# Branch A's attention: three of eight units of each group turned by VectorE's 32x32 blocks and a DMA through DRAM instead of by TensorE

## The chip, the cores and the metric

The kernel runs on one core of one Trainium2 chip. Its time is the device time of one execution in microseconds (us); 2126.03 us is the median of three runs before the change (2126.02 to 2127.18).

The engines that matter here are TensorE (PE in the profile: matrix products and transposes, with its weight loads on a row of their own, PEld), VectorE (DVE), ScalarE (ACT), GpSimd (POOL), SyncE (SP, which issues most DMAs) and the DMA queues. Tiles lie in on-chip memory (SBUF) and products are summed in PSUM banks of 128 x 512 floats.

## The reference, cut to what matters

One layer with two token mixers, for a sample of 512 tokens and a prompt of 1024 tokens, 1024 channels wide. Branch A is attention with eight query heads of 64 in two groups, each group sharing one head of keys and values:

```python
z = rmsnorm(x) @ W_in        # q_A k_A v_A q_B k_B v_B gate_A gate_B
q, k = rope(headnorm(q_A)), rope(headnorm(k_A))
s   = einsum('bqkgd,bskd->bkgqs', q_block, k) * 64**-0.5    # 128 queries at a time
p   = softmax(s, axis=-1)
o_a = einsum('bkgqs,bskd->bqkgd', p, v)
mix = (sigmoid(gate_A) * (o_a @ W_pA) + sigmoid(gate_B) * (o_b @ W_pB)) @ W_out
x   = x + mix
x   = x + relu(rmsnorm(x) @ W_up)**2 @ W_down
```

All of it is in 32-bit floats. The kernel gets a float product out of TensorE's rounded operands by splitting an operand into a rounded part (`hi`) and the remainder (`lo`): a product of two split operands is three matmuls (`mm3`), hi x hi, hi x lo and lo x hi.

## The kernel before, in words

The program walks through the sample first, then the prompt, then the two-matrix block behind both. Inside one sequence (`N` is 0 for the sample, 1 for the prompt) branch A goes group by group: a phase `phR` projects, normalises and rotates queries, keys and values, and a phase `phA` does the attention. Branch B (`phB`), the output projections and the rest follow. In the profile of before, the prompt's two `phA` phases lie at about 460 to 600 us and 640 to 780 us.

In `phA` of the prompt the work is cut into eight units of 512 queries (4 heads x 2 query blocks, numbered 0 to 7 below). A unit has

- four score tiles (`s_tile`, j = 0 to 3), each of 128 queries x 1024 keys: four matmuls of 512 columns into a PSUM tile `s` of two banks (two such tiles exist), a maximum over the row on DVE, the exponential on ACT with the row's sum as a by-product, the reciprocal on DVE, and the scaling of the row on POOL. The result is `p`, 128 queries x 1024 keys in SBUF (eight such buffers).
- eight key blocks (kc = 0 to 7). The second product needs keys on the partitions, so for each block TensorE transposes the 128 x 128 piece of each of the four `p` tiles into one PSUM bank `pT` (128 keys x 512 queries); ACT copies the bank as `hi`, DVE subtracts to get `lo`, and two matmuls (`pv`) of 512 columns add both into the output bank `o`, two blocks later (`LAG = 2`).

`pT`, `o` and the gate's product take turns in a pool of four PSUM banks. In the course of one unit's blocks TensorE also does the next unit's score tiles (at blocks 0, 1, 3 and 4) and, block by block, three matmuls of another product, the gate's columns (`fill.pull(1)`; `fill` is a Python generator that emits three matmuls for each step; what is left of it at the end of a group is emitted by `fill.drain()`). Loads of the gate's weights (`raw_gs`) come over the SP queue and are split into `w_gs` by ACT and DVE. When a unit's last `pv` is out, `finish_o` adds the two halves of `o` (`ot` on ACT, `os` on DVE), and `put` stores the sum.

The order of the instructions on each engine is set by a scheduler when the kernel is built; where the code says `tc.keep_in_program_order(op)`, the instruction stays behind those before it that are held in the same way. Before the change nothing in the prompt's `phA` is held. `mul` and `mm3` hold their matmuls whenever the list `held_pe` isn't empty, which before is so only in a part of branch B. `put` issues a store at once, on ACT's queue, as long as `slot_no[0]` is `None`; with a number there it keeps the store in a list, `later_put`, until the program issues it on SP's queue.

Branch B already turns a part of its probabilities without TensorE, and its rows are used below: `pbs` is turned in 32x32 blocks by DVE (L1100), written to DRAM (`tbs`), fetched (`bhs`), and `bhs` is rounded by ACT (L1122) and DVE (L1123). Its exponential (L1088) writes runs of 32 where the tile is turned in this way, and single floats four apart where it is not.

## Time and profile before

| | before |
|---|---|
| median of three runs | 2126.03 us (2126.02 to 2127.18) |
| time of the profiled execution | 2126.34 us |
| span of the profiled execution | 2124.5 us |
| PE busy | 2096.5 us, 99% of the span |
| PEld busy | 1839.0 us, 87% |
| DVE busy | 1480.0 us, 70% |
| ACT busy | 1145.7 us, 54% |
| POOL busy | 363.3 us, 17% |

The span is the time from the first to the last instruction on the chip; the execution's own time is 1.84 us longer. In rows of groups of instructions, "A<-B" is what an instruction writes and reads, then come the shape in partitions x elements, the number of instructions after an x, the busy time with the mean of one in ns, and behind the second bar the engine's idle time just before such instructions with what ended it. In rows of the timeline the first number is the start in us and the second the duration; matmuls overlap in PE's pipe, so that the pace of a row of them is the distance of their starts. L12 is line 12 of the kernel.

### The profile page before, as it was taken

Reading aid. Unit: us, or ns where it says so; the run is one execution under the profiler, and the core shown is the slowest. Engines: PE = TensorE matmul, PEld = TensorE weight load, DVE = VectorE, ACT = ScalarE, POOL = GpSimd, SP = SyncE. Lnnn points to the kernel's source line nnn. Section 1 sums busy time; section 2 is a strip of 40 time slices with the busy share of each in tenths; the row PEclk is TensorE's granted clock in tenths of the full one; section 3 lists DMA queues with packets and bytes.
Section 4 is the critical chain, followed back from the end, with each engine's and each line's share of the span. In section 5 each row is a group of like instructions: output and inputs, shape, how many; then the busy total and the mean of one; then the engine's idle time right before and its main releaser. Section 6 shows DMA issues by size and latency. Waiting matters only on the chain.

```text
span 2124.5 us, 31728 instructions
## 1 busy us (share of the span) xinstructions
PE 2096.5 (99%) x10871; PEld 1839.0 (87%) x10871; DVE 1480.0 (70%) x2793; ACT 1145.7 (54%) x2487; POOL 363.3 (17%) x446
## 2 busy tenths in 40 slices
PE   9999999999999999999999999999999999999998
PEld 8888778888898888887888999999999988888887
DVE  6666786777647756777873877778777777669563
ACT  6665653666666745556531566666565643334452
POOL 2232310332232314443101100002000000000000
PEclk9999999999999999999999999999999999999999
DMA  6436557530122136876563656568454899688561
GB/s 191 133 99 200 160 150 256 192 86 23 49 70 87 45 84 193 241 224 193 172 227 124 199 181 206 163 230 214 156 162 146 272 350 341 213 280 278 164 204 64
DMA packets 336104, 372.92 MB, mean 176 GB/s; under 512 B 31039, under 2 KB 267207, under 8 KB 335943
## 3 DMA queue, kind: packets, MB, share of 16 engines
q1 hardware_dynamic: 297463, 305.60, 45.6%
q10 hardware_dynamic: 31328, 45.11, 6.2%
q0 software_dynamic: 7152, 20.19, 3.5%
q8 instruction: 86, 1.41, 0.3%
q14 instruction: 75, 0.61, 0.1%
HBM read 274.29 MB, written 97.32 MB: 175 GB/s over the span
## 4 chain that ended last, share of the span: by engine, by line
PE 52%; DVE 1%; issue 0%; ACT 0%; POOLq 0%; POOL 0%; ACTq 0%; DVEq 0%
PE dn L212 20%; PE ua L212 6%; PE ud L212 6%; PE uc L212 6%; PE ops L212 4%; PE ub L212 3%; PE ppbs L212 2%; PE ppas L212 2%; PE dnf L212 2%; PE pt L353 1%; PE obs L212 0%; PE ptbs L1132 0%; ACT pbs L1088 0%; PE sbs L212 0%; DVE A L1458 0%
## 5 line engine op out<-in xcount | busy, mean ns | idle before, releaser
L212 PE MATMUL dn<-wd,ah 128*128 128x512 f32 x1248 | 384.2, 389 | 0.0
L212 PEld LDWEIGHTS dn<-wd,ah 128*128 128x128 f32 x1248 | 234.2, 188 | 48.7
L212 PE MATMUL dn<-wd,al 128*128 128x512 f32 x624 | 242.8, 389 | 0.0
L1457 ACT ACTIVATE ah<-ar 128x512 fp32r<-128x512 f32 x168 | 104.4, 627 | 206.7 <-PE dn L212 185.6
L212 PE MATMUL gpss<-xs_0h,w_gs 128*128 128x512 f32 x512 | 189.4, 402 | 0.8 <-DVE ot_Bs L471 0.4
L1458 DVE TENSOR_TENSOR al<-ar,ah 128x512 fp32r<-128x512 f32 x168 | 114.1, 687 | 76.4 <-ACT ah L1457 66.6
L212 PE MATMUL ud<-B,A 128*128 128x384 f32 x768 | 143.7, 334 | 0.7 <-DVE c L1575 0.7
L212 PE MATMUL uc<-B,A 128*128 128x384 f32 x768 | 143.7, 334 | 0.0
L212 PE MATMUL ua<-B,A 128*128 128x384 f32 x768 | 138.8, 334 | 0.0
L212 PEld LDWEIGHTS dn<-wd,al 128*128 128x128 f32 x624 | 117.1, 188 | 24.2
L794 POOL TENSOR_SCALAR ps<-ps,rls 128x1024 f32<-128x1024 f32 (+1 forms) x96 | 96.8, 1009 | 228.4 <-DVE rls L793 213.8
L212 PEld LDWEIGHTS ud<-B,A 128*128 128x128 f32 x768 | 134.0, 188 | 1.1 <-DVE c L1575 1.1
L212 PEld LDWEIGHTS uc<-B,A 128*128 128x128 f32 x768 | 134.1, 188 | 0.2 <-ACT A L1457 0.2
L834 ACT ACTIVATE pths<-pTs 128x512 fp32r<-128x512 f32 x160 | 94.1, 597 | 73.9 <-PE pTs L829 71.3
L212 PEld LDWEIGHTS ua<-B,A 128*128 128x128 f32 x768 | 133.7, 188 | 0.2
L835 DVE TENSOR_TENSOR ptls<-pTs,pths 128x512 fp32r<-128x512 f32 x160 | 107.5, 686 | 37.7 <-ACT pths L834 36.7
L212 PE MATMUL ops<-wh_os,mgs 128*128 128x512 f32 x384 | 119.4, 390 | 0.0
L788 DVE TENSOR_REDUCE nms<-ss 128x1 f32<-128x1024 f32 (+1 forms) x96 | 99.8, 1040 | 25.0 <-PE ss L786 24.5
L212 PEld LDWEIGHTS gpss<-xs_0h,w_gs 128*128 128x128 f32 x512 | 96.1, 188 | 19.0 <-DVE w_gs L206 0.7
L791 ACT ACTIVATE ps<-ss,nms 128x1024 f32<-128x1024 f32 (+1 forms) x96 | 93.3, 972 | 32.1 <-DVE nms L788 26.2
L180 POOL TENSOR_TENSOR rs_f<-ms_f,mhalf 128x1 f32<-128x1 f32 x6 | 4.0, 667 | 590.7 <-DVE ms_f L176 590.7
L829 PEld LDWEIGHTS pTs<-ident,ps 128*128 128x128 f32 x640 | 78.0, 140 | 28.4 <-POOL ps L794 4.4
(287 smaller groups left out, 5144.2 us busy)
## 6 DMA issues: line engine op xcount, KB each, us to landing
ar<-ud SPq DMA_DIRECT2D x120, 512.0 KB, 5.4
br<-in_w_mlp_down_dram SPq DMA_DIRECT2D x72, 512.0 KB, 5.3
rawu<-in_w_mlp_up_dram SPq DMA_DIRECT2D x64, 512.0 KB, 4.1
ud<-c ACTq DMA_DIRECT2D x128, 192.0 KB, 3.6
raw_gs<-in_w_in_dram SPq DMA_DIRECT2D x32, 512.0 KB, 3.9
ud<-cs SPq DMA_DIRECT2D x64, 192.0 KB
tbs<-pbs SPq DMA_DIRECT2D x24, 384.0 KB, 4.8
bhs<-tbs SPq DMA_DIRECT2D x24, 384.0 KB, 3.7
```

Source lines behind the costliest of these rows:

```text
L180: nc.gpsimd.tensor_tensor(r[:, :n], m[:, :n], mhalf[:, :n], op=ALU.pow)
L212: op = nc.tensor.matmul(out, a, b, **kw)
L353: nc.tensor.transpose(halves[c // 4][:, (c % 4) * P : (c % 4 + 1) * P], t[:, c * P : (c + 1) * P], ident)
L788: nc.vector.tensor_reduce(nm_, s, axis=AX.X, op=ALU.max, negate=True)
L791: op = nc.scalar.activation(p, s, AF.Exp, bias=nm_, accum_out=l)
L794: nc.gpsimd.tensor_scalar(p, p, rl, 1.0, op0=ALU.mult, op1=ALU.mult)
L829: nc.tensor.transpose(pt[:, j * P : (j + 1) * P], PP[u, j][:, kc * P : (kc + 1) * P], ident)
L834: nc.scalar.activation(hi, pt, AF.Copy)
L835: nc.vector.tensor_tensor(lo, pt, hi.bitcast(F32), op=ALU.subtract)
L1457: nc.scalar.activation(hi, src, AF.Copy)
L1458: nc.vector.tensor_tensor(lo, src, hi.bitcast(F32), op=ALU.subtract)
```

## The change

In both groups of the prompt, units 1, 3 and 5 are "turned": TensorE no longer transposes their probabilities. For such a unit

- the exponential reads the scores in another order, with a step of four floats in PSUM, and writes runs of 32 floats, so that the 32x32 blocks come to lie side by side (L798 to L803 of the changed kernel);
- DVE turns each of the four 128 x 1024 tiles in place in 32x32 blocks (`turn`, L832), and SP stores the tile to DRAM (512 KB, L834);
- SP fetches it again in another order of partitions (`fetch`, 512 KB, L841), which completes the transposition;
- ACT makes the rounded copy (128 x 1024, L848, not before the last exponential issued so far), and the remainder is formed in place (L850), for tiles j = 0 and 2 on POOL, for j = 1 and 3 on DVE (`rounded`);
- `pv_pair` takes two tiles at a time: 16 matmuls of 256 columns for each of a unit's two halves.

So five units have their eight blocks: `step` for units 0, 2, 4, 6 and 7, and `between_steps` where a turned unit is. In `between_steps` TensorE does the four score tiles of the unit after, the last two `pv` of the unit before, four steps of the gate's product and the first half of the turned unit; the second half comes at block 1 of the following step. The score tiles of a turned unit are done at blocks 0 to 3 of the step before it. All of TensorE's matmuls of the phase are held in program order, and so are DVE's turns, SP's stores and fetches, and the subtractions of `rounded`. A `p` buffer now holds two tiles, and four such pairs are shared by `p` and the fetched `fa`. The outputs' stores go by `later_put` on SP's queue. Nothing changes for the sample and for the rest but line numbers.

The diff, with `pv`, `end_o`, the issue of the late stores and what only changes how functions are called left out:

```diff
 ...
@@ -772,9 +772,10 @@
                 setup_bias()
             with phase(f"phA{N}_{g}") as ph:
                 units = [(h, qb) for h in range(4) for qb in range(NB)]
-                PP = {}
-
-                def s_tile(u, j):
+                PP, tA, fA, hA, pairs, last_exp = {}, {}, {}, {}, {}, [None]
+                turned = {units[i] for i in (1, 3, 5)} if NB == 2 else set()
+
+                def s_tile(u, j, between=None):
                     h, qb = u
                     nm = f"{N}_{g}_{h}_{qb}_{j}"
                     q0 = (qb * 4 + j) * P
 ...
-                    p = ph.tile([P, T], F32, tag="P", name=f"p{nm}", bufs=8)
+                    if between is not None:
+                        between()
+                    if NB == 1:
+                        p = ph.tile([P, T], F32, tag="P", name=f"p{nm}", bufs=8)
+                    else:
+                        if j % 2 == 0:
+                            pairs[u, j // 2] = ph.tile([P, 2, T], F32, tag="P", name=f"p{nm}", bufs=4)
+                        p = pairs[u, j // 2][:, j % 2]
                     l = sml.tile([P, 1], F32, tag="l", name=f"l{nm}")
-                    op = nc.scalar.activation(p, s, AF.Exp, bias=nm_, accum_out=l)
+                    to, of = p, s
+                    if u in turned:
+                        to = p.rearrange("p (b k i) -> p k b i", b=4, i=32)
+                        of = s.rearrange("p (k i b) -> p k b i", b=4, i=32)
+                    op = nc.scalar.activation(to, of, AF.Exp, bias=nm_, accum_out=l)
+                    last_exp[0] = op.ins
                     rl = sml.tile([P, 1], F32, tag="rl", name=f"rl{nm}")
                     nc.vector.reciprocal(rl, l)
                     nc.gpsimd.tensor_scalar(p, p, rl, 1.0, op0=ALU.mult, op1=ALU.mult)
 ...
+                def turn(u, j):
+                    p = PP[u, j]
+                    blocks = p.rearrange("p (n i) -> p n i", i=32)
+                    tc.keep_in_program_order(nc.vector.transpose(blocks, blocks))
+                    tA[u, j] = dram.tile([P, 4, T // 4], F32, name=f"ta{N}_{g}_{u[0]}_{u[1]}_{j}")
+                    tc.keep_in_program_order(nc.sync.dma_start(tA[u, j], p.rearrange("p (b w) -> p b w", b=4)))
+
+                def fetch(u, j):
+                    of = tA.pop((u, j)).rearrange("(a i) b w -> (i b) a w", i=32)
+                    if j % 2 == 0:
+                        fA[u, j // 2] = ph.tile([P, 2, T], F32R, tag="P", name=f"fa{N}_{g}_{u[0]}_{u[1]}_{j}", bufs=4)
+                    to = fA[u, j // 2][:, j % 2].bitcast(F32).rearrange("p (a w) -> p a w", a=4)
+                    tc.keep_in_program_order(nc.sync.dma_start(to, of))
+
+                def rounded(u, j, eng):
+                    if j % 2 == 0:
+                        hA[u, j // 2] = slot([P, 2, T], F32R, f"ha{N}_{g}_{u[0]}_{u[1]}_{j // 2}")
+                    p, hi = fA[u, j // 2][:, j % 2], hA[u, j // 2][:, j % 2]
+                    with tc.issue_after(last_exp[0]):
+                        nc.scalar.activation(hi, p.bitcast(F32), AF.Copy)
+                    tc.keep_in_program_order(
+                        eng.tensor_tensor(p, p.bitcast(F32), hi.bitcast(F32), op=ALU.subtract)
+                    )
+
+                def pv_pair(u, pr):
+                    if pr == 0:
+                        o_of[u] = mm(f"o{N}_{g}_{u[0]}_{u[1]}")
+                    o = o_of[u][:, pr * 256 : pr * 256 + 256].rearrange("p (n i) -> p n i", i=32)
+                    hi, lo = hA.pop((u, pr)), fA.pop((u, pr))
+                    for kc in range(NT):
+                        for i, t in enumerate((hi, lo)):
+                            mv = t.rearrange("p j w -> p (j w)").rearrange("p (n k i) -> p k n i", n=8, i=32)[:, kc]
+                            mul(
+                                o,
+                                vhl[:, kc, :],
+                                mv,
+                                start=(kc + i == 0),
+                                stop=(kc + i == NT),
+                                skip_group_check=True,
+                            )
+                    if pr == 1:
+                        end_o(u)
+
+                if NB == 2:
+                    held_pe.append("A")
+                    slot_no[0] = 0
 ...
+                def put_later():
+                    slot_no[0] += 1
+                    while later_put and later_put[0][0] < slot_no[0] - 1:
+                        nc.sync.dma_start(*later_put.pop(0)[1:])
+
+                def step(u, nxt, late, pulls):
+                    h, qb = u
+                    moving = nxt in turned
+                    if moving:
+                        after = {4: [partial(fetch, nxt, 0)], 5: [partial(turn, nxt, 3), partial(fetch, nxt, 1)]}
+                        after[7] = [partial(fetch, nxt, 2), partial(rounded, nxt, 0, nc.gpsimd)]
+                    for kc in range(NT):
+                        pt = mm(f"pT{N}_{g}_{h}_{qb}_{kc}")
+                        for j in range(4):
+                            op = nc.tensor.transpose(
+                                pt[:, j * P : (j + 1) * P], PP[u, j][:, kc * P : (kc + 1) * P], ident
+                            )
+                            tc.keep_in_program_order(op)
+                        hi = ph.tile([P, 512], F32R, tag="pth", name=f"pth{N}_{g}_{h}_{qb}_{kc}", bufs=3)
+                        lo = ph.tile([P, 512], F32R, tag="ptl", name=f"ptl{N}_{g}_{h}_{qb}_{kc}", bufs=3)
+                        nc.scalar.activation(hi, pt, AF.Copy)
+                        nc.vector.tensor_tensor(lo, pt, hi.bitcast(F32), op=ALU.subtract)
+                        queue.append((u, kc, hi, lo))
+                        if nxt is not None:
+                            at = (0, 1, 2, 3) if moving else (0, 1, 3, 4)
+                            if kc in at:
+                                j = at.index(kc)
+                                s_tile(nxt, j, partial(turn, nxt, j - 1) if moving and j else None)
+                            for f in after.get(kc, ()) if moving else ():
+                                f()
+                        fill.pull(pulls[kc])
+                        if kc == 1 and late is not None:
+                            pv_pair(late, 1)
+                        if len(queue) > LAG:
+                            pv(*queue.pop(0))
+                        if kc % 4 == 3:
+                            put_later()
+
+                def between_steps(u, nxt):
+                    s_tile(nxt, 0)
+                    pv(*queue.pop(0))
+                    fetch(u, 3)
+                    s_tile(nxt, 1)
+                    pv(*queue.pop(0))
+                    fill.pull(2)
+                    s_tile(nxt, 2, partial(rounded, u, 1, nc.vector))
+                    fill.pull(1)
+                    rounded(u, 2, nc.gpsimd)
+                    s_tile(nxt, 3)
+                    fill.pull(1)
+                    rounded(u, 3, nc.vector)
+                    pv_pair(u, 0)
+                    put_later()
+
+                if NB == 2:
+                    for i in (0, 2, 4):
+                        step(units[i], units[i + 1], units[i - 1] if i else None, (1,) * 8)
+                        between_steps(units[i + 1], units[i + 2])
+                    step(units[6], units[7], units[5], (2, 1, 1, 1, 1, 1, 1, 2))
+                    step(units[7], None, None, (2, 1, 1, 1, 1, 1, 1, 2))
 ...
```

What this makes of the engines' orders is shown at two places. Names end in sequence, group, head, query block and tile or key block: `ps_0_1_1_2` is tile 2 of group 0, head 1, query block 1, which is unit 3, a turned one; unit 2 is `0_1_0` and unit 4 is `0_2_0`. `ps` is the scaled tile, `nms` the row maximum, `rls` the reciprocal, `ptls` the remainder of a transposed block; `fas` and `has` are the fetched and the rounded tile. After the change two tiles share a buffer that is named for the first, so that `ps_0_1_1_0` stands for tiles 0 and 1, and `fas_0_1_1_0` likewise.

The first is the step of unit 2, in which the tiles of unit 3 are made. DVE there, before:

```order
L788 TENSOR_REDUCE nms_0_1_1_1_6061<-ss_0_1_1_1_6056 128x1
L793 RECIPROCAL rls_0_1_1_0_6039<-ls_0_1_1_0_6037 128x1
L483 TENSOR_TENSOR os_As_0_0_1_6076<-os_0_0_1_5923,ot_As_0_0_1_6074 64x512
L835 TENSOR_TENSOR ptls_0_1_0_2_6085<-pTs_0_1_0_2_6079,pths_0_1_0_2_6084 128x512
L793 RECIPROCAL rls_0_1_1_1_6066<-ls_0_1_1_1_6064 128x1
L788 TENSOR_REDUCE nms_0_1_1_2_6108<-ss_0_1_1_2_6103 128x1
L835 TENSOR_TENSOR ptls_0_1_0_3_6100<-pTs_0_1_0_3_6094,pths_0_1_0_3_6099 128x512
L835 TENSOR_TENSOR ptls_0_1_0_4_6124<-pTs_0_1_0_4_6118,pths_0_1_0_4_6123 128x512
L788 TENSOR_REDUCE nms_0_1_1_3_6132<-ss_0_1_1_3_6127 128x1
```

and now:

```order
L806 RECIPROCAL rls_0_1_1_0_5991<-ls_0_1_1_0_5989 128x1
L832 STREAM_TRANSPOSE ps_0_1_1_0_5988<-ps_0_1_1_0_5988 128x1024
L806 RECIPROCAL rls_0_1_1_1_6018<-ls_0_1_1_1_6016 128x1
L483 TENSOR_TENSOR os_As_0_0_1_6042<-os_0_0_1_5955,ot_As_0_0_1_6040 64x512
L902 TENSOR_TENSOR ptls_0_1_0_2_6050<-pTs_0_1_0_2_6044,pths_0_1_0_2_6049 128x512
L789 TENSOR_REDUCE nms_0_1_1_2_6058<-ss_0_1_1_2_6053 128x1
L832 STREAM_TRANSPOSE ps_0_1_1_0_5988<-ps_0_1_1_0_5988 128x1024
L902 TENSOR_TENSOR ptls_0_1_0_3_6081<-pTs_0_1_0_3_6075,pths_0_1_0_3_6080 128x512
L806 RECIPROCAL rls_0_1_1_2_6066<-ls_0_1_1_2_6064 128x1
L789 TENSOR_REDUCE nms_0_1_1_3_6089<-ss_0_1_1_3_6084 128x1
L832 STREAM_TRANSPOSE ps_0_1_1_2_6063<-ps_0_1_1_2_6063 128x1024
L902 TENSOR_TENSOR ptls_0_1_0_4_6112<-pTs_0_1_0_4_6106,pths_0_1_0_4_6111 128x512
```

The turns now stand between the remainders of the blocks; the turn of tile 0 stands ahead of the remainder of block 2, the turn of tile 1 ahead of that of block 3, and that of tile 2 ahead of block 4's.

The second place is `between_steps` at unit 3. POOL there; before:

```order
L794 TENSOR_SCALAR ps_0_1_1_3_6134<-ps_0_1_1_3_6134,rls_0_1_1_3_6137 128x1024
L794 TENSOR_SCALAR ps_0_2_0_0_6203<-ps_0_2_0_0_6203,rls_0_2_0_0_6206 128x1024
L794 TENSOR_SCALAR ps_0_2_0_1_6234<-ps_0_2_0_1_6234,rls_0_2_0_1_6237 128x1024
L794 TENSOR_SCALAR ps_0_2_0_2_6281<-ps_0_2_0_2_6281,rls_0_2_0_2_6284 128x1024
L794 TENSOR_SCALAR ps_0_2_0_3_6305<-ps_0_2_0_3_6305,rls_0_2_0_3_6308 128x1024
```

and now:

```order
L850 TENSOR_TENSOR fas_0_1_1_0_6115<-fas_0_1_1_0_6115,has_0_1_1_0_6171 128x1024
L807 TENSOR_SCALAR ps_0_2_0_0_6187<-ps_0_2_0_0_6187,rls_0_2_0_0_6190 128x1024
L807 TENSOR_SCALAR ps_0_2_0_0_6187<-ps_0_2_0_0_6187,rls_0_2_0_1_6205 128x1024
L807 TENSOR_SCALAR ps_0_2_0_2_6232<-ps_0_2_0_2_6232,rls_0_2_0_2_6235 128x1024
L850 TENSOR_TENSOR fas_0_1_1_2_6169<-fas_0_1_1_2_6169,has_0_1_1_1_6241 128x1024
L807 TENSOR_SCALAR ps_0_2_0_2_6232<-ps_0_2_0_2_6232,rls_0_2_0_3_6253 128x1024
```

Two subtractions of 128 x 1024 now stand on POOL among the scalings of unit 4's tiles, the second of them ahead of the scaling of tile 3.

DVE there; before, while unit 4's tiles 2 and 3 are made:

```order
L835 TENSOR_TENSOR ptls_0_1_1_2_6256<-pTs_0_1_1_2_6250,pths_0_1_1_2_6255 128x512
L835 TENSOR_TENSOR ptls_0_1_1_3_6271<-pTs_0_1_1_3_6265,pths_0_1_1_3_6270 128x512
L788 TENSOR_REDUCE nms_0_2_0_2_6279<-ss_0_2_0_2_6274 128x1
L835 TENSOR_TENSOR ptls_0_1_1_4_6295<-pTs_0_1_1_4_6289,pths_0_1_1_4_6294 128x512
L788 TENSOR_REDUCE nms_0_2_0_3_6303<-ss_0_2_0_3_6298 128x1
L793 RECIPROCAL rls_0_2_0_2_6284<-ls_0_2_0_2_6282 128x1
L835 TENSOR_TENSOR ptls_0_1_1_5_6325<-pTs_0_1_1_5_6319,pths_0_1_1_5_6324 128x512
```

and now:

```order
L789 TENSOR_REDUCE nms_0_2_0_2_6228<-ss_0_2_0_2_6223 128x1
L806 RECIPROCAL rls_0_2_0_1_6205<-ls_0_2_0_1_6203 128x1
L483 TENSOR_TENSOR os_As_0_1_0_6212<-os_0_1_0_6072,ot_As_0_1_0_6210 64x512
L850 TENSOR_TENSOR fas_0_1_1_0_6115<-fas_0_1_1_0_6115,has_0_1_1_0_6171 128x1024
L806 RECIPROCAL rls_0_2_0_2_6235<-ls_0_2_0_2_6233 128x1
L789 TENSOR_REDUCE nms_0_2_0_3_6249<-ss_0_2_0_3_6244 128x1
L806 RECIPROCAL rls_0_2_0_3_6253<-ls_0_2_0_3_6251 128x1
L850 TENSOR_TENSOR fas_0_1_1_2_6169<-fas_0_1_1_2_6169,has_0_1_1_1_6241 128x1024
```

Of unit 3's blocks, one `ptls` for each, nothing is left here; the maximum of unit 4's tile 3 stands behind the remainder of the fetched tile 1, and the reciprocal of tile 2 ahead of that maximum. TensorE does one step of the gate's product and the first half of unit 3 between unit 4's last score tile and the first transposes that read it, where before blocks 4 to 7 of unit 3 stood.

28 lines of the change are left out of this document (19 added, 9 removed).

## The prediction

> **What bounds the kernel now.** I read the page's busy shares and chain of waits first, then windows inside the two phases that change, then the waits of TensorE there, and last the timeline.
>
> ```profile
> span 2124.5 us, 31728 instructions
> PE 2096.5 (99%) x10871; PEld 1839.0 (87%) x10871; DVE 1480.0 (70%) x2793; ACT 1145.7 (54%) x2487; POOL 363.3 (17%) x446
> 480.00:500.00 20.00, 20.00 (x109) 16.36 (x108) 14.94 (x24) 13.31 (x24) 5.41 (x5) 1.00 0.07 21
>   DVE os_As L483: 3.1, 12
>   POOL ps L794: 2.0, 5
>   DVE ptls L835: 1.0, 4
> ```
>
> TensorE is busy in the whole of the 20 us window (PE is its first figure, then PEld, DVE, ACT, POOL, the granted clock, which is full, and DMA's share), with DVE at 14.94 us second. The last three rows are what ended the waits of the transposes (L829) from 440 to 780 us, both phases together: 6.1 us. So TensorE's own work sets the pace, a matmul saved there is time saved, and any wait that the change brings is time lost.
>
> **What leaves TensorE.**
>
> ```profile
> 480.66 0.60 PE L829 MATMUL pTs<-ident,ps 128*128 128x128 f32 x4
> 481.01 0.48 PE L785 MATMUL ss<-kTs,qTs 128*128 128x512 f32 x1
> 481.33 0.40 PE L786 MATMUL ss<-kTs,qTs 128*128 128x512 f32 x1
> 481.56 0.40 PE L785 MATMUL ss<-kTs,qTs 128*128 128x512 f32 x1
> 481.80 0.40 PE L786 MATMUL ss<-kTs,qTs 128*128 128x512 f32 x1
> 482.03 0.39 PE L212 MATMUL gpss<-xs_0h,w_gs 128*128 128x512 f32 x1
> 864.73 0.89 PE L212 MATMUL obs<-bhs,vss 128*128 128x256 f32 x6
> 865.45 0.87 PE L212 MATMUL sbs<-kBs,qBs 128*128 128x384 f32 x4
> ```
>
> Starts tell the pace. The four transposes of a block take 481.01 - 480.66 = 0.35 us; the matmul behind them 0.32 where the others take 0.23; a block's transposes thus cost 0.35 + 0.09 = 0.44. Six turned units have 48 blocks: -21.1 us. Their second product becomes 32 matmuls of 256 columns instead of 16 of 512. Six of 256 take 865.45 - 864.73 = 0.72, so 0.12 each: 32 x 0.12 - 16 x 0.2315 = +0.14 a unit, +0.8 us. Net **-20.3 us**, or 3.4 for a pair of an unturned and a turned unit; that is what a pair may wait before nothing is won.
>
> **What comes onto DVE and POOL.**
>
> ```profile
> L835 DVE TENSOR_TENSOR ptls<-pTs,pths 128x512 fp32r<-128x512 f32 x160 | 107.5, 686 | 37.7 <-ACT pths L834 36.7
> L788 DVE TENSOR_REDUCE nms<-ss 128x1 f32<-128x1024 f32 x64 | 77.9, 1217 | 17.6 <-PE ss L786 17.5
> L1100 DVE STREAM_TRANSPOSE pbs<-pbs 128x768 f32<-128x768 f32 x24 | 23.2, 966 | 0.0
> L1123 DVE TENSOR_TENSOR bhs<-bhs 128x768 fp32r<-128x768 f32 x24 | 23.1, 964 | 9.9 <-ACT bhs L1122 9.7
> L834 ACT ACTIVATE pths<-pTs 128x512 fp32r<-128x512 f32 x160 | 94.1, 597 | 73.9 <-PE pTs L829 71.3
> L791 ACT ACTIVATE ps<-ss,nms 128x1024 f32<-128x1024 f32 x64 | 71.3, 1115 | 21.3 <-DVE nms L788 15.4 <-DMA vds<-vts 3.1 <-DVE rls L793 2.5
> L794 POOL TENSOR_SCALAR ps<-ps,rls 128x1024 f32<-128x1024 f32 x64 | 73.6, 1150 | 170.2 <-DVE rls L793 167.0 <-PE pTs L829 3.2
> L365 POOL TENSOR_TENSOR B<-ta,B 128x512 fp32r<-128x512 f32 x12 | 15.5, 1294 | 120.6 <-ACT B L362 120.2
> L685 POOL TENSOR_TENSOR us<-ts,rts 128x160 f32<-128x160 f32 x48 | 29.3, 632 | 56.3 <-issue 30.0 <-DVE vhls L677 20.2 <-DVE ts L676 6.1
> ```
>
> By length, a turn of 1024 takes 0.966 x 1024/768 = 1.29 and a subtraction on DVE 1.28. A turned unit gives DVE four turns and two subtractions for eight remainders of 0.69: +7.7 - 5.5 = +2.2 us. A pair keeps its TensorE work else: 16 blocks at 0.44 + 0.46, eight score tiles at 0.93 and twelve gate steps of three matmuls at 0.69 are 30.1 us before, and 26.8 now. DVE has 14.94/20 x 30.1 = 22.5 before, some 24.7 now: from 75% to 92%. It still fits, but nothing on it can be late for long. A subtraction of 1024 on POOL isn't in the trace; its two nearest rows give (1.294 - 0.632)/352 = 1.88 ns a column and so 1.294 + 512 x 0.00188 = 2.26; in proportion to either row it is 2.6 or 4.0, at the scalings' pace 1.15. I take 2.3, as the row of 512 is nearest.
>
> **The wait inside a step** (three of a group's steps make a turned unit's tiles). Two of four PSUM banks are free for `pT`, since `o` and the gate's product hold the others: block k's transposes wait for the remainder of block k-2.
>
> ```profile
> 482.54 1.22 DVE L788 TENSOR_REDUCE nms<-ss 128x1 f32<-128x1024 f32 x1
> 483.67 0.15 DVE L793 RECIPROCAL rls<-ls 128x1 f32<-128x1 f32 x1
> 485.73 0.16 DVE L793 RECIPROCAL rls<-ls 128x1 f32<-128x1 f32 x1 [0.40 <-ACT ps L791]
> 486.06 1.12 POOL L794 TENSOR_SCALAR ps<-ps,rls 128x1024 f32<-128x1024 f32 x1 [0.95 <-DVE rls L793]
> ```
>
> Now the first turn stands ahead of block 2's remainder. From the step's start it can't begin before 6.7 us: remainder 0 and maximum 0 end at 3.2, the exponential (behind ACT's second copy) at 4.5, maximum 1 and the reciprocal at 5.3, and the scaling runs from 0.33 later for 1.1. To block 4's remainder DVE then has turn 1.29, reciprocal 0.16, `os` 0.68, remainder 0.69, maximum 1.22, turn 1.29, remainder 0.69, reciprocal 0.16, maximum 1.22, turn 1.29, remainder 0.69: 9.4, or 8.7 since an instruction starts some 0.08 before the stated end of the one ahead (482.54 + 1.22 against 483.67). It ends at 15.4 to 16.1. Block 6's transposes wait for it, and TensorE would reach them at 14.3 (six blocks with four tiles, six gate steps, four `pv` and 1.93 for half a turned unit): 1.1 to 1.8, and I take 1.2. In a group's first step that half unit and the `os` are missing: TensorE is there at 12.3, the remainder at 14.7 to 15.4, and I take 2.7. Without this late turn both would be 0. Sum 4 x 1.2 + 2 x 2.7 = **+10.2 us**.
>
> **The wait between steps.** Here the last score tile S3 of the next unit is followed on TensorE by only one gate step (0.69) and half a turned unit (1.93), and then by block 0's transposes, the fourth of which reads S3's scaled tile. Counting from the end of tile S2 on: DVE maximum 2 to 1.2, reciprocal 1, `os` to 2.1, the subtraction of fetched tile 1 to 3.3, reciprocal 2 to 3.5, so that S2's scaling goes from 3.7 to 4.8 on POOL. Then POOL's second subtraction stands ahead of S3's scaling: to 7.1, and that scaling to 8.3. TensorE has gate 0.69, S3 0.93, gate 0.69 and the half 1.93, with the start of the next row in its pipe 4.4. The wait is 3.9; the three pairs of a group differ by which reciprocal stands behind which subtraction (3.3, 3.8, 4.6 by the same walk), so 4.0 x 6 = **+24 us**. Below, only S3's own chain remains (maximum 1.22, exponential and reciprocal 1.23, scaling 0.33 + 1.12 with hand-overs, 4.4 from S3's last matmul against 3.2 of work): 1.15 x 6 = 7. Above, 5 x 6 = 30, if POOL's and DVE's subtractions of two SBUF tiles hinder each other:
>
> ```profile
> 811.52 1.18 POOL L1091 TENSOR_SCALAR pbs<-pbs,rlbs 128x384 f32<-128x384 f32 x2 [1.26 <-DVE rlbs L1090]
> 826.70 1.84 POOL L1091 TENSOR_SCALAR pbs<-pbs,rlbs 128x384 f32<-128x384 f32 x2 [1.77 <-DVE rlbs L1090]
> 827.12 0.97 DVE L1123 TENSOR_TENSOR bhs<-bhs 128x768 fp32r<-128x768 f32 x1
> ```
>
> Two scalings take 1.18 alone and 1.84 beside such a subtraction: +0.66. [...]
>
> **What is hidden, and the end.** A store and a fetch of 512 KB each pass on SP between TensorE's blocks:
>
> ```profile
> raw_gs<-in_w_in_dram SPq DMA_DIRECT2D x3, 512.0 KB, 4.2
> tbs<-pbs SPq DMA_DIRECT2D x24, 384.0 KB, 4.8
> bhs<-tbs SPq DMA_DIRECT2D x24, 384.0 KB, 3.7
> ```
>
> At 4.2 each the first fetched tiles land some 9 us after their turns (7 to 13 us into the step), in time for the copies behind the next unit's first exponential; the DMA share was 0.07. ACT loses 56 rows and isn't late; On SP each fetch waits for its tile's store; behind it stand the next stores, the outputs' stores moved here, which nothing in the phase reads, and loads of the gate's weights, which come a column block ahead. The gate's steps run out after block 2 of a group's last unit; its five blocks are then bound by transposes, copy 0.60 and remainder 0.69, about 1 us a group more: +2.
>
> **Sum.** 2124.5 - 20.3 + 24 + 10.2 + 2 = 2140.4; with 2126.34 - 2124.5 = 1.84 around the span 2142.2, and the profiled execution lies 0.31 above the median: 2142.
>
> **Rivals.** *The waits are small* (the other side): TensorE's saving stays and only S3's own chain is waited for. It speaks for it that DVE and POOL are idle at times and that the walk adds up gaps which overlap; against it that both orders above are held. 2126 - 20.3 + 7 = 2113 with steps at 0. It decides when a pair waits under 3.4. *No change*: a pair waits about 3.4 in all (say 2.5 between and 0.9 in the step), 2126. *The strided exponential*: a turned unit's exponential reads every fourth float of PSUM.
>
> ```profile
> L1088 ACT ACTIVATE pbs<-sbss,nmbs 128x384 f32<-128x384 f32 x14 | 13.7, 996 | 7.4 <-DVE nmbs L1059 7.3
> L1088 ACT ACTIVATE pbs<-sbss,nmbs 128x384 f32<-128x384 f32 x50 | 31.1, 625 | 19.4 <-DMA tbs<-pbs 13.0 <-issue 2.8 <-DVE nmbs L1059 2.8
> ```
>
> From 985 to 1050 us branch B's exponential writes single floats four apart and takes 0.996, from 780 to 985 it writes runs of 32 and takes 0.625: +0.37 for 384 floats, so +1.0 for 1024. The tile's turn would be later by that, and the step's wait by about 1 a pair: +6, 2148. For the rest reads may differ from writes, and no row has such a read. [...] *Late fetches*: at 4.9 a transfer, the copies on ACT stand late ahead of the next exponential; 0.75 a pair, +4.5, 2146.5.
>
> **Chances.** The forecast's mechanism, waits in both places above the saving (2131 to 2150), has 0.50; the small waits 0.19; no change 0.11; the strided exponential 0.13; late fetches 0.07. About 0.2%, or 4.3 us, can be told from no change; so faster 0.19, same 0.11, slower 0.70. The range reaches down to 2116, into the small waits, and up to 2152, where the strided read and hindered subtractions come together; the likeliest case's own is 2131 to 2150.
>
> **What would show it.** Right: 96 matmuls of 128x256 more and 96 transposes fewer in a group, at 0.12 each and 0.44 a block; first transposes of units 2, 4, 6 idle 3 to 5 us with POOL's scaling as releaser; in steps, transposes idle with DVE's remainder as releaser, and the turns late by POOL. Wrong: PE still 99% busy in both phases; a POOL subtraction near 1.2; the exponential of turned units near 2 us; transposes released by a DMA.

## The result: slower by 1.7%, more than twice what was forecast

| | before | with the change |
|---|---|---|
| median | 2126.61 us (2126.02 to 2127.59, 4 runs) | 2163.35 us (2160.54 to 2164.4, 4 runs) |
| ratio | | 1.0170 (95%: 1.0153 to 1.0188) |
| span of the profiled execution | 2124.5 us | 2161.7 us |

The kernel became 36.7 us slower. The forecast was 2142 us (2116 to 2152): the direction was right, but the time lies above the range, and the loss is 37 us where 16 were forecast. The spans differ by 37.2 us.

The profile's page of the changed kernel, first rows of the busy times:

```profile
span 2161.7 us, 31545 instructions
PE 2092.8 (97%) x10775; PEld 1835.1 (85%) x10775; DVE 1499.9 (69%) x2781; ACT 1143.7 (53%) x2463; POOL 403.9 (19%) x458
```

TensorE is no longer busy throughout. The two phases in windows, first before, then with the change (columns as before: length, PE, PEld, DVE, ACT, POOL, granted clock, DMA share, GB/s):

```profile
453.00:580.00 127.00, 126.17 (x676) 102.90 (x676) 92.70 (x147) 84.08 (x149) 36.98 (x32) 1.00 0.14 43
640.00:780.00 140.00, 139.91 (x746) 114.78 (x745) 96.04 (x153) 88.92 (x162) 37.24 (x33) 1.00 0.21 61
```

```profile
455.00:600.00 145.00, 124.81 (x634) 102.17 (x632) 102.64 (x140) 84.36 (x136) 57.15 (x38) 0.95 0.38 124
655.00:815.00 160.00, 139.32 (x717) 114.50 (x716) 109.78 (x154) 89.15 (x151) 58.60 (x41) 0.96 0.43 136
```

Before, TensorE stood still for under 1 us in a phase, at a clock of 1.00. Now it stands still for 145 - 124.8 = 20.2 and 160 - 139.3 = 20.7 us, and the clock's mean is 0.95 and 0.96. TensorE's waits from 440 to 820 us, with what ended them, the total, the number and the longest:

```profile
PE pTs L895 <- POOL ps L807: 27.9, 10, 4.1
PE os L212 <- issue: 6.0, 6, 1.7
PE pTs L895 <- DVE ptls L902: 3.5, 6, 0.8
PE ss L212 <- ACT ps L803: 2.6, 3, 0.9
PE pTs L895 <- DVE os_As L483: 1.0, 1, 1.0
```

Of the ten waits in the first row six stand between steps and four at the groups' starts. One of the six, on TensorE, at units 3 and 4 of the first group (L212 is the helper `mul`, through which all matmuls but the transposes go):

```profile
525.26 0.28 PE L212 MATMUL os<-has,vhls 128*128 128x256 f32 x1
526.55 0.36 PE L212 MATMUL os<-fas,vhls 128*128 128x256 f32 x1 [1.01 <-issue]
...
528.43 0.49 PE L895 MATMUL pTs<-ident,ps 128*128 128x128 f32 x3
532.97 0.33 PE L895 MATMUL pTs<-ident,ps 128*128 128x128 f32 x1 [4.05 <-POOL ps L807]
```

and on POOL and DVE at the same place:

```profile
528.51 2.34 POOL L850 TENSOR_TENSOR fas<-fas,has 128x1024 fp32r<-128x1024 f32 x1
530.83 2.08 POOL L807 TENSOR_SCALAR ps<-ps,rls 128x1024 f32<-128x1024 f32 x1
...
525.24 1.20 DVE L850 TENSOR_TENSOR fas<-fas,has 128x1024 fp32r<-128x1024 f32 x1
...
528.91 0.16 DVE L806 RECIPROCAL rls<-ls 128x1 f32<-128x1 f32 x1 [1.27 <-ACT ps L803]
529.86 2.07 DVE L850 TENSOR_TENSOR fas<-fas,has 128x1024 fp32r<-128x1024 f32 x1 [0.78 <-ACT has L848]
```

Three of four transposes are out at 528.4; the fourth waits 4.05 us for the scaling of the last score tile. Its reciprocal is there at 529.1, but POOL is at its subtraction until 530.85, and then the scaling itself takes 2.08 in place of 1.12, beside a DVE subtraction that takes 2.07 in place of 1.20. That is the forecast's mechanism. Two things beside it were not in the forecast: half a turned unit waits inside itself (1.01 at 526.55, until the DVE subtraction of 525.24 is over), and what comes behind the long wait is slow. Three windows around the same wait one pair earlier, and TensorE's rows behind it:

```profile
496.00:500.00 4.00, 1.39 (x6) 1.17 (x7) 1.90 (x2) 0.60 (x1) 2.55 (x2) 0.95 0.00 0
500.00:504.00 4.00, 4.00 (x14) 3.25 (x14) 2.63 (x4) 1.69 (x3) 0.00 (x0) 0.62 0.03 6
504.00:508.00 4.00, 4.00 (x28) 3.68 (x28) 2.67 (x6) 2.40 (x4) 1.59 (x2) 1.00 0.00 0
```

```profile
499.75 0.63 PE L212 MATMUL gpss<-xs_1h,w_gs 128*128 128x512 f32 x1
500.18 0.63 PE L212 MATMUL gpss<-xs_1l,w_gs 128*128 128x512 f32 x1
```

The matmuls start 0.43 apart instead of 0.23, and the granted clock is 0.50 for some 3.4 us. Taking the windows in slices of half a microsecond and adding up (1 - clock) x busy time gives 6.8 us in the first group (four such stretches) and 5.9 in the second (three), none before.

**Where the 37.2 us are.** TensorE's idle time is 40.9 us in the two phases, against 0.9 before: +40.0. The low clock: +12.6. A wait costs more than its row says, because the idle time begins at the end of the last matmul's 0.28 to 0.39, not at the pace of 0.12 or 0.23: at 526.55 the starts lie 1.29 apart, 1.17 more than the pace, for a row of 1.01. About 0.2 for each of 26 waits of more than 0.15 is +5.2. With TensorE's saving of -20.3 as forecast the sum is 37.5. The 0.2 is an estimate from rows like this one, so the parts are good to a microsecond or two.

### The profile page after: what moved, and what is told of

Same layout as the page of the kernel before. It is cut to its first block, busy times and chain, and to the rows that moved or that the text cites. A ratio compares the mean times of both kernels' runs of the same rounds, so it can differ in the third digit from the quotient of the medians.

```text
span 2161.7 us, 31545 instructions
## 1 busy us (share of the span) xinstructions
PE 2092.8 (97%) x10775; PEld 1835.1 (85%) x10775; DVE 1499.9 (69%) x2781; ACT 1143.7 (53%) x2463; POOL 403.9 (19%) x458
## 4 chain that ended last, share of the span: by engine, by line
PE 52%; DVE 1%; issue 0%; ACT 0%; POOLq 0%; POOL 0%; ACTq 0%; DVEq 0%
PE dn L212 20%; PE ua L212 6%; PE ud L212 6%; PE uc L212 6%; PE ops L212 4%; PE ub L212 3%; PE ppbs L212 2%; PE ppas L212 2%; PE dnf L212 2%; PE pt L353 0%; PE obs L212 0%; PE gpss L212 0%; PE sbs L212 0%; PE ptbs L1263 0%; DVE A L1589 0%
## 5 line engine op out<-in xcount | busy, mean ns | idle before, releaser
L212 PE MATMUL dn<-wd,ah 128*128 128x512 f32 x1248 | 384.4, 389 | 0.0
L212 PEld LDWEIGHTS dn<-wd,ah 128*128 128x128 f32 x1248 | 234.2, 188 | 48.7
L212 PE MATMUL dn<-wd,al 128*128 128x512 f32 x624 | 242.8, 389 | 0.0
L212 PE MATMUL gpss<-xs_0h,w_gs 128*128 128x512 f32 x512 | 190.0, 405 | 0.8 <-DVE ot_Bs L471 0.4
L807 POOL TENSOR_SCALAR ps<-ps,rls 128x1024 f32<-128x1024 f32 (+1 forms) x96 | 108.7, 1134 | 197.5 <-DVE rls L806 123.6
L212 PE MATMUL ud<-B,A 128*128 128x384 f32 x768 | 143.6, 334 | 0.7 <-DVE c L1706 0.7
L212 PE MATMUL uc<-B,A 128*128 128x384 f32 x768 | 143.7, 334 | 0.0
L212 PE MATMUL ua<-B,A 128*128 128x384 f32 x768 | 138.8, 334 | 0.0
L212 PEld LDWEIGHTS dn<-wd,al 128*128 128x128 f32 x624 | 117.1, 188 | 24.3
L212 PEld LDWEIGHTS ud<-B,A 128*128 128x128 f32 x768 | 134.0, 188 | 1.0 <-DVE c L1706 1.0
L212 PEld LDWEIGHTS uc<-B,A 128*128 128x128 f32 x768 | 134.0, 188 | 0.2 <-ACT A L1588 0.2
L212 PEld LDWEIGHTS ua<-B,A 128*128 128x128 f32 x768 | 133.7, 188 | 0.2
L212 PE MATMUL ops<-wh_os,mgs 128*128 128x512 f32 x384 | 119.4, 390 | 0.0
L212 PEld LDWEIGHTS gpss<-xs_0h,w_gs 128*128 128x128 f32 x512 | 97.7, 191 | 19.9 <-DVE w_gs L206 0.7
L803 ACT ACTIVATE ps<-ss,nms 128x1024 f32<-128x1024 f32 (+1 forms) x96 | 93.3, 973 | 34.8 <-DVE nms L789 31.2
L212 PE MATMUL ss<-kTs,qTs 128*128 128x512 f32 x320 | 100.4, 429 | 5.1 <-ACT ps L803 3.3
L212 PE MATMUL gpss<-xs_0l,w_gs 128*128 128x512 f32 x256 | 101.8, 398 | 0.0
L212 PE MATMUL gpss<-xs_1h,w_gs 128*128 128x512 f32 x256 | 95.9, 410 | 0.0
```

Source lines behind the costliest of these rows:

```text
L212: op = nc.tensor.matmul(out, a, b, **kw)
L803: op = nc.scalar.activation(to, of, AF.Exp, bias=nm_, accum_out=l)
L807: nc.gpsimd.tensor_scalar(p, p, rl, 1.0, op0=ALU.mult, op1=ALU.mult)
```

## The experiments

All times are medians beside runs of the kernel before on the same chip (2126.8 to 2127.1). The theory at this point: POOL's and DVE's subtractions stand ahead of the scaling that TensorE waits for, and the wait lowers the clock behind it. The rivals: the own chain of the last score tile; the held order of TensorE; a saving that was priced too high. In the edits, `rounded(..., sub=False)` is ACT's copy alone and `rounded(..., copy=False)` the subtraction alone, which then stays behind the instruction named in the comment or in `after_`.

### POOL's second subtraction behind the scaling

```diff
-                    rounded(u, 2, nc.gpsimd)
+                    rounded(u, 2, nc.gpsimd, sub=False)      # ACT's copy only
                     s_tile(nxt, 3)
+                    rounded(u, 2, nc.gpsimd, copy=False)     # POOL, behind the scaling of tile 3
```

> The changed kernel with one instruction moved: POOL's second subtraction (fetched tile 2) is issued behind the scaling of the next unit's tile 3 instead of ahead of it. Theory (POOL's queue, then the clock): the wait of 4.05 us ahead of the next unit's first transposes loses about the subtraction's 2.35 and comes to 1.5 to 2; at that length the granted clock stays at 1.00 behind it. 6 x (2.3 + 1.7) = 24 less than 2163: 2139 (2133 to 2147). Rival (DVE and tile 3's own chain end last, POOL only happens to be the last in the row): the wait stays above 3.4 and the time at 2158 to 2164.

Measured: 2145.62 us (2142.11 to 2146.95), 17.7 less than the change. TensorE and POOL at the same place as above:

```profile
526.32 0.49 PE L902 MATMUL pTs<-ident,ps 128*128 128x128 f32 x3
528.24 0.33 PE L902 MATMUL pTs<-ident,ps 128*128 128x128 f32 x1 [1.43 <-POOL ps L808]
...
527.07 1.12 POOL L808 TENSOR_SCALAR ps<-ps,rls 128x1024 f32<-128x1024 f32 x1 [1.43 <-DVE rls L807]
528.15 3.36 POOL L855 TENSOR_TENSOR fas<-fas,has 128x1024 fp32r<-128x1024 f32 x1
```

The wait falls from 4.05 to 1.43, and the clock stays at 1.00 behind all six. POOL's subtraction is what stood in the way. A part of the gain is given back: in the last pair of each group a new wait of 3.16 and 3.08 us appears, for `os`, with a low clock behind it. DVE there has splits of weights for what follows the group, ahead of `os`; the first of them takes 2.89 and 2.88 beside POOL's late subtraction (3.37 and 3.38).

### Useless matmuls in the wait

Ahead of block 0's transposes in the steps that follow a turned unit, 16 matmuls of 512 columns are put in, whose result is overwritten:

```diff
                         pt = mm(f"pT{N}_{g}_{h}_{qb}_{kc}")
+                        if kc == 0 and late is not None:
+                            for _ in range(16):
+                                mul(pt, kT[:, 0, 0:P], kT[:, 1, 0:512], start=True, stop=True)
```

> The changed kernel with 16 matmuls of 512 columns, whose result is overwritten, ahead of the first transposes of units 2, 4, 6 and, at the group's end, of none else (about 3.7 us of TensorE's time put into the wait of 4.05). Theory (a long wait lowers the granted clock for the 3.5 us behind it): the wait falls under 1 us, the transposes start when they did, the clock stays at 1.00, and the matmuls behind run at 0.23 instead of 0.43: about 1.7 x 6 = 10 us less, 2153 (2149 to 2157), though more work is done. Rival (the slow matmuls behind the wait have another cause, or the clock falls whatever TensorE does): 2163 or more.

Measured: 2155.24 us (2154.37 to 2156.01), 8.1 less with 22 us of work more. At the first pair:

```profile
494.63 3.84 PE L212 MATMUL pTs<-kTs 128*128 128x512 f32 x16
498.31 0.49 PE L898 MATMUL pTs<-ident,ps 128*128 128x128 f32 x3
499.23 0.33 PE L898 MATMUL pTs<-ident,ps 128*128 128x128 f32 x1 [0.42 <-POOL ps L807]
499.31 1.18 PE L212 MATMUL ss<-kTs,qTs 128*128 128x512 f32 x4
500.33 0.39 PE L212 MATMUL gpss<-xs_1h,w_gs 128*128 128x512 f32 x1
500.55 0.39 PE L212 MATMUL gpss<-xs_1l,w_gs 128*128 128x512 f32 x1
```

The transpose comes no later against its surroundings, the matmuls behind it run at 0.23, and the only low clock that is left is at the first group's start. The low clock is caused by the wait and is worth 8 to 10 us of the 37.

### DVE's second subtraction out of POOL's way

```diff
-                    rounded(u, 3, nc.vector)
+                    rounded(u, 3, nc.vector, sub=False)
 ...
                         queue.append((u, kc, hi, lo))
+                        if kc == 0 and late is not None:
+                            rounded(late, 3, nc.vector, copy=False)   # behind block 0's remainder
```

> The changed kernel with one instruction moved: DVE's second subtraction (fetched tile 3) stands behind the remainder of block 0 of the next step instead of beside POOL's scaling of tile 3. Theory (the two hinder each other): the scaling of tile 3 falls from 2.1 to 1.15 us, DVE's subtraction from 2.07 to 1.2, the wait from 4.05 to 3.1: 6 us less, 2157, and 2147 if a wait of 3.1 no longer lowers the clock. Rival (the scaling is long for another reason): scaling and time as they were, 2163; or the half unit that needs this tile now waits and the time rises.

Measured: 2155.96 us (2153.91 to 2160.72). POOL and DVE at the first pair:

```profile
492.49 2.33 POOL L857 TENSOR_TENSOR fas<-fas,has 128x1024 fp32r<-128x1024 f32 x1
494.81 1.11 POOL L808 TENSOR_SCALAR ps<-ps,rls 128x1024 f32<-128x1024 f32 x1
...
497.78 1.22 DVE L855 TENSOR_TENSOR fas<-fas,has 128x1024 fp32r<-128x1024 f32 x1
```

The subtraction takes 1.22 instead of 2.07, the scaling 1.11 instead of 2.1 in four of the six pairs, and their waits are 3.07 or less. So the two do hinder each other, by 1 us a pair. In the last pair of each group the scaling stays at 2.07 and 2.08, now beside DVE's splits of weights, and the waits are 3.26 and 3.25. The time lies between the two values expected, but close to the upper: the waits between steps are 5.8 us less in all, while TensorE's idle time from 440 to 820 us falls by only 2.2 (41.4 to 39.2), since other waits grow. More of the gain is the clock's, which still falls behind three of the six waits and costs 5.8 instead of 12.6 us.

### TensorE's order held, nothing turned

`turned` is empty; all eight units go through `step`, with score tiles at blocks 0, 1, 3 and 4 and the gate steps as before the change.

```diff
-                turned = {units[i] for i in (1, 3, 5)} if NB == 2 else set()
+                turned = set()
 ...
+                    for i, u in enumerate(units):
+                        step(u, units[i + 1] if i < 7 else None, None, (1, 1, 1, 0, 1, 1, 1, 0))
```

> The changed kernel with no unit turned: eight steps of blocks as before, score tiles at blocks 0, 1, 3 and 4 and gate steps as before, but TensorE's order held, stores on SP and pairs of tiles in a buffer. Theory: holding the order costs only the waits at each group's start (2 us, with a low clock behind it in one group) and little inside: 2129 to 2134. Rival (the held order is itself what costs, since the scheduler can no longer fill gaps): over 2145.

Measured: 2132.74 us (2131.04 to 2137.45), ratio 1.0028 (1.0018 to 1.0038): the held order costs 5.6 us. (The run also keeps the stores on SP and two tiles in a buffer; no run tells their share apart.) The loss stands at the groups' starts: 4.1 us of waits, and 3.4 of low clock in the profiled execution. There TensorE waits for the scalings of tiles 2 and 3, and the clock falls behind them in both groups:

```profile
462.71 0.38 PE L895 MATMUL pTs<-ident,ps 128*128 128x128 f32 x2
464.11 0.33 PE L895 MATMUL pTs<-ident,ps 128*128 128x128 f32 x1 [1.02 <-POOL ps L807]
465.48 0.33 PE L895 MATMUL pTs<-ident,ps 128*128 128x128 f32 x1 [1.04 <-POOL ps L807]
```

Before the change the scheduler had put the next unit's score matmuls and gate steps between these very transposes:

```profile
462.99 0.38 PE L829 MATMUL pTs<-ident,ps 128*128 128x128 f32 x2
463.12 0.48 PE L785 MATMUL ss<-kTs,qTs 128*128 128x512 f32 x1
...
464.39 0.33 PE L829 MATMUL pTs<-ident,ps 128*128 128x128 f32 x1
464.47 0.47 PE L212 MATMUL gpss<-xs_1h,w_gs 128*128 128x512 f32 x1
```

### More work behind the first score tiles

```diff
                     ends = s_tile(units[0], j)
-                    fill.pull(2)
+                    fill.pull((1, 2, 1, 4)[j] if NB == 2 else 2)
```

> The changed kernel, with the gate steps behind a group's first four score tiles dealt out as 1, 2, 1, 4 instead of 2, 2, 2, 2, so that TensorE has 2.8 us of work behind the fourth tile instead of 1.4. Theory (the wait at a group's start, twice 1.02 us in each group, is tile 3's own chain against what TensorE has left): about 1.0 to 1.4 less per group, with some new wait ahead of tile 2 of 0.4, and no low clock behind it: 2163 - 2 x 0.8 - 1.7 = 2160 (2157 to 2162). Rival (the start's waits come from something else): the same two waits of 1.02, 2163.

Measured: 2161.94 us (2159.67 to 2163.74). In each group one wait of 0.92 is left of the two, as the theory had it, but the medians differ by 1.4 us where each kernel's runs spread over 4: the direction is not settled by the times.

### Everything that stands between the scaled tiles and the second product left out

```diff
                 def turn(u, j):
-                    ...
+                    pass
 
                 def fetch(u, j):
-                    ...
+                    pass
 
                 def rounded(u, j, eng):
-                    ...
+                    if (u, j // 2) not in fA:
+                        fA[u, j // 2] = hA[u, j // 2] = same[0]   # two tiles of unit 0, rounded once
```

> The changed kernel with everything left out that a turned unit needs between its scaled tiles and its second product: DVE's turns, the stores, the fetches, the rounded copies and all four subtractions (the second products read two tiles of unit 0 rounded once in place of the fetched ones, so that the outputs of units 1, 3 and 5 are not the reference's). TensorE's instructions and their order are those of the changed kernel. Theory (TensorE's saving is 20.3 us as priced, and tile 3's own chain leaves a wait of about 1.2, with some 0.2 more that a row of idle time does not show, between the steps): 2126.8 + 7.2 (start of the groups, as in the run with the order held alone) - 20.3 + 6 x 1.4 + 2 (gate steps run out at the end) = 2124 (2119 to 2129). Rival (the saving on TensorE was priced too high, and is nearer to 13): 2131 or more.

Measured: 2123.06 us (2121.33 to 2125.14), 4.0 less than the kernel before. TensorE from 440 to 820 us, which holds both phases, here and with the order held alone (the run with no unit turned, above), columns as before; this run first:

```profile
440.00:820.00 380.00, 367.11 (x2016) 316.36 (x2015) 226.33 (x416) 214.82 (x503) 111.69 (x114) 0.99 0.26 73
440.00:820.00 380.00, 374.41 (x2062) 318.72 (x2061) 247.40 (x445) 230.72 (x535) 106.92 (x108) 0.99 0.24 66
```

This run is 9.7 us shorter than the order held alone, although TensorE idles 12.9 instead of 5.6 us, the low clock costs 1.3 more (4.75 and 3.41, in slices as above) and six more waits cost 0.2 each: 9.7 + 7.3 + 1.3 + 1.2 = 19.5 for a saving that was priced at 20.3. The price holds to within 1 us; the saving is not where the 37 came from. And even with nothing to do for DVE, POOL and the DMAs between the tiles, the last score tile's own chain leaves waits of 0.7 to 0.9 between steps. This run's own two copies of unit 0's tiles, which stand on ACT between the first exponentials, lengthen the groups' starts: waits of 2.17 and then 0.77 or 0.62 stand there in place of 1.02 and 1.04, 1.6 us more in all, and the 1.3 of low clock come on top. So with TensorE's order as it is some 4 + 3 = 7 us were to be gained at most, an estimate from these rows.

### TensorE's order left to the scheduler

```diff
-                    held_pe.append("A")
 ...
-                            op = nc.tensor.transpose(
+                            nc.tensor.transpose(
                                 pt[:, j * P : (j + 1) * P], PP[u, j][:, kc * P : (kc + 1) * P], ident
                             )
-                            tc.keep_in_program_order(op)
```

> The changed kernel, but TensorE's order is left to the scheduler as it was before the change (turns, stores, fetches and subtractions stay held). Theory (the waits come from what DVE, POOL and ACT do ahead of the transposes, and these orders are nearly the same): the long waits between the steps stay in part, 2145 to 2165, since the scheduler does move gate steps and products into the gaps but not the scaling of tile 3 ahead of POOL's subtraction. Rival (holding TensorE's order is itself the fault): under 2135.

Measured: 2136.94 us (2135.51 to 2138.2), ratio 1.0048 (1.0031 to 1.0065) to the kernel before. That is 26.4 less than the change, with nothing undone but the hold on TensorE's order. The time lies below the theory's range and above the rival's: the order is a larger part of the loss than I had stated here, and not all of it. TensorE's waits from 455 to 815 us:

```profile
PE pTs L894 <- POOL ps L807: 15.2, 8, 3.0
PE os L212 <- DVE fas L850: 1.7, 2, 0.9
```

POOL's row is still there with 15.2 of 27.9. In four of the six pairs (waits of 2.47, 2.95, 2.55 and 3.04) the scaling still stands behind the held subtraction; in the second pair of each group the waits (0.4 and 1.73) are for earlier tiles' scalings. What is gone are the waits at the start, in the steps and most of those inside half a unit, and a good part of each long one, since score matmuls and gate steps are put into it. The clock falls behind four waits instead of seven.

### Rearranged, with the order held and with it free

Between the steps, score tiles 2 and 3 follow each other, three gate steps stand behind them, POOL's second subtraction stands behind the scaling of tile 3, DVE's first behind the reciprocal of tile 2 and its second behind block 0's remainder; `pv_pair` does its eight products with the rounded part first; the start is 1, 2, 1, 4; the splits of the second group's weights come behind block 3 of unit 6.

```diff
                     pv(*queue.pop(0))
-                    fill.pull(2)
-                    s_tile(nxt, 2, partial(rounded, u, 1, nc.vector))
-                    fill.pull(1)
-                    rounded(u, 2, nc.gpsimd)
-                    s_tile(nxt, 3)
                     fill.pull(1)
-                    rounded(u, 3, nc.vector)
+                    rounded(u, 1, nc.vector, sub=False)
+                    s_tile(nxt, 2)
+                    rcp2 = last_rcp[0]
+                    s_tile(nxt, 3, partial(rounded, u, 1, nc.vector, copy=False, after_=rcp2))
+                    rounded(u, 2, nc.gpsimd, sub=False)
+                    rounded(u, 2, nc.gpsimd, copy=False, after_=last_scale[0])
+                    rounded(u, 3, nc.vector, sub=False)
+                    fill.pull(3)
                     pv_pair(u, 0)
```

> All 48 blocks are still turned, but the waits found so far are worked against together: between the steps the next unit's score tiles 2 and 3 directly follow each other and three gate steps stand behind tile 3; POOL's second subtraction stands behind the scaling of tile 3, DVE's first behind the reciprocal of tile 2, DVE's second behind the remainder of block 0 of the next step; half a turned unit does its eight products with the rounded part first; the gate steps of a group's start are 1, 2, 1, 4; and the splits of the second group's weights stand behind block 3 of unit 6. Theory: the wait ahead of the first transposes falls under 1 us, the wait inside half a unit to near 0, the waits in the steps (about 0.8 to 1 each) and the start (1 to 1.5 a group) stay, and the clock no longer falls: 2126 + 1 (order held) - 20.3 + 6 x 1 + 6 x 1 + 3 = 2122 (2116 to 2130). Rival (DVE and ACT are simply full in these stretches, so that waits only move elsewhere): over 2135.

Measured with the order held: 2135.14 us (2132.68 to 2138.12), ratio 1.0037 (1.0024 to 1.0050), 28.2 less than the change but above the range expected. The waits between steps are 0.3 to 0.5 now, but others stand elsewhere: 5.8 us in six at score tiles (0.66 to 1.65), for the exponential of a tile before, 4.3 in six at transposes, for a remainder, and 2.8 in two for `os`. In a fixed order TensorE meets each of them.

> The rearranged kernel (both subtractions moved, score tiles 2 and 3 together, rounded part first, start and weight splits moved) with TensorE's order left to the scheduler. Theory: with the instructions of the other engines in a good order, the scheduler's freedom removes the wait at the groups' start (about 3 us with the low clock) and some of the waits of 0.3 to 1.6 us at score tiles, and costs nothing: 2126 to 2133. Rival (the scheduler's own estimates of DVE and ACT are off here and it brings transposes too early): over 2137.

Measured with the order free: 2120.68 us (2119.73 to 2121.34), ratio 0.9969 (0.9958 to 0.9981); below the expected range. The page and the waits of the two phases:

```profile
span 2119.3 us, 31543 instructions
PE 2081.1 (98%) x10775; PEld 1823.7 (86%) x10775; DVE 1488.9 (70%) x2781; ACT 1142.1 (54%) x2463; POOL 396.9 (19%) x458
...
PE pTs L901 <- POOL ps L808: 4.5, 8, 0.8
PE pTs L901 <- DVE ptls L907: 2.2, 2, 1.1
PE ss L212 <- ACT ps L804: 1.8, 2, 1.0
```

Some 10 us of waits are left, and the clock is 1.00 throughout. Run again:

> The rearranged kernel with TensorE's order free once more, with more rounds, beside the one above on the same chip: 2120.7 as before (2119.5 to 2122), which is 6 us less than the kernel before the change. If it were luck of one chip or of one build: within 4 us of 2127.

Measured: 2120.3 us (2119.76 to 2122.83, 8 runs), ratio 0.9971 (0.9961 to 0.9982). This version is faster than the kernel before the change, by 6.5 us or 0.3%.

### One move, with the order free

The first experiment and the free order together, to see whether that is enough:

> The changed kernel with two things undone: TensorE's order is left to the scheduler, and POOL's second subtraction stands behind the scaling of tile 3. With TensorE's order free, the subtraction's place still leaves waits of 2.1 to 3.0 us ahead of the first transposes in all six pairs (15.2 us in all) and a low clock behind four of them. Theory (the two faults are separate, and each of the two places is paid for by itself): those waits fall to about 1 us, the clock stays full: 2136.9 - 6 x 1.5 - 6.6 = 2121 (2118 to 2126). Rival (with the order free the scheduler has already given away what there is, and DVE's remaining order decides): 2131 or more.

Measured: 2128.57 us (2127.37 to 2130.98), ratio 1.0009 (1.0000 to 1.0018): neither the theory's 2121 nor the rival's 2131. The long waits are gone except for one of 1.73 in each group (with a low clock behind it), but others take their place: 2.7 us for POOL's subtraction, which is now late for the second half of a unit in the last pair (1.34 and 1.36), and 4.2 inside halves of units. Moving one instruction passes the lateness on to what was behind it.

All six together, median in us:

| | TensorE's order held | left to the scheduler |
|---|---|---|
| as changed | 2163.35 | 2136.94 |
| POOL's subtraction moved | 2145.62 | 2128.57 |
| rearranged | 2135.14 | 2120.68 |

The two causes overlap: moving the late subtraction is worth 17.7 us where TensorE's order is held and 8.4 where TensorE may do something else meanwhile, and the held order costs 26.4 us in the changed kernel but 5.6 where no unit is turned.

## Why the prediction was right or wrong

- **What leaves TensorE: right, to within 1 us.** -20.3 us forecast, 19.5 found with the rounding left out. (The 6.1 us of waits in the text's first fence count those of the weight loads too; before the change TensorE's matmuls idled 1.4 us in all from 440 to 820 us.)
- **The durations: right for instructions undisturbed, not beside each other.** POOL's subtraction of 1024 columns was taken as 2.3 and took 2.34 to 2.41, DVE's turn as 1.29 and took 1.20 to 1.25, its subtraction as 1.28. The first subtraction of a unit took 1.20 to 1.23, but the second, beside POOL, 1.93 to 2.83, and the scaling of tile 3 2.1 for 1.12. (ACT's loss of 56 rows in the text isn't borne out by the pages: its instructions fall by 24, from 2487 to 2463.)
- **The wait between steps: the mechanism right, the size at the upper bound.** 24 us were forecast, with 30 as the upper end. POOL's subtraction ahead of the last scaling as the cause is shown by the first experiment. The first transposes wait 4.05 us four times and 3.8 twice, 23.8 in all, but 6.0 more in six stand ahead of them inside half a turned unit, where the walk had let DVE's subtraction end at 3.3 and TensorE come to it at 2.3 and had counted no wait of its own for the difference. The later wait didn't become shorter for it, since the scaling came later too: in the pair shown it let the transposes go 10.0 us after the end of tile 2 (523.0), not 8.3. Of these 1.7, 1.0 is POOL and DVE hindering each other: DVE's second subtraction, issued at 529.86 while POOL's runs to 530.85, takes 2.07, and POOL's scaling behind it 2.08, where they take 1.22 and 1.11 apart. The other 0.7 had come in before: tile 2's scaling ended 5.5 after the end of tile 2, not 4.8, since it and tile 1's took 3.71 together, beside DVE's first subtraction. The forecast had chosen the case without hindrance. With the waits inside the half the trace has 29.8, next to the 30 given for the case with it, though it is luck that the figures are so close: the 5 a pair behind the 30 was the author's estimate, with no wait inside the half, and no row of before showed the hindrance between two such subtractions (the one shown was +0.66 on two scalings).
- **The wait inside a step: too large.** 10.2 forecast; the transposes' waits for a remainder are 3.5 in six. In the first step of each group 2.7 was forecast and 0.78 came: the text had taken the first turn to stand ahead of block 2's remainder, as it does in the order shown for unit 2's step, but in the first steps it stands behind it, and from its start to the end of block 4's remainder DVE takes 6.1 (682.15 to 688.2). In the other four steps 1.2 was forecast and 0.37 to 0.75 came; DVE took 8.5 in the second pair (506.16 to 514.69), a little less than the 8.7 to 9.4 given. With the useless matmuls, where the clock stayed full, these four waits are 0.72 to 0.76.
- **The end of a group: absent.** 2 forecast; no wait stands there.
- **The groups' start: not priced.** The change holds TensorE's order, and the text priced the order as it stands without asking what the scheduler had done with these gaps before. That is 5.6 us by itself, with no unit turned, and it is also what lets each later wait count in full: with the order free the same change costs 10 instead of 37.
- **The clock: not priced, the largest single omission.** The sum took every duration at the clock of 1.00 that its first window showed, and added the waits as waits. Seven stretches of low clock cost 12.6 us; filling the wait with useless work gave back 8. The wait of 4 us was forecast, the loss with it was not: a fall came with each of the six, at about 1.7 for 3.4 us at 0.50, which would have made the forecast 2142 + 6 x 1.7 = 2152. The trace of before does not show it: TensorE's longest wait there, 2.1 us at 975.5, left the clock at 1.00. What the traces of the changed kernel and of the experiments say of it stands at the end.
- **The strided exponential: refuted.** The exponentials of turned units read every fourth float of PSUM and write runs of 32. They take as long as the others: all 64 exponentials of the two phases take 1.10 to 1.12. Of the two rows the first is in a step that makes a turned unit's tiles, the second between steps:

```profile
509.86 1.12 ACT L803 ACTIVATE ps<-ss,nms 128x1024 f32<-128x1024 f32 x1
520.62 1.10 ACT L803 ACTIVATE ps<-ss,nms 128x1024 f32<-128x1024 f32 x1
```

  So a strided read of PSUM with runs of 32 written costs nothing here, and the penalty that branch B's rows showed is left to the strided write, which no run here tests by itself. The +1.0 for the read was the author's estimate from these writes; no row of before had such a read.
- **Late fetches: there, but small.** The text had the first fetched tile in time. ACT's first copy of each turned unit waited for its fetch, 1.05 to 2.49 us, 10.6 in six. Behind the three longest of these (2.33 to 2.49) TensorE waits at a score tile for an exponential, 2.6 us in all.

The waits' own total came out near only because errors cancel: 24 + 10.2 + 2 = 36.2 us were forecast and 40.9 are found, with the step and the end of a group too large, and the half unit and the groups' starts left out. The steps that failed are thus the sum's silent one, that a wait costs only its own length at an unchanged clock (12.6 us of low clock and some 5 that no row of idle time shows came on top), and the missing price of a held order (5.6 us by itself, 26.4 in the changed kernel).
